# One decoder step: sample attention by column groups, and a pre-norm stage by token tiles in an order fixed by hand

## The chip, the cores and the metric

The kernel runs on one core of one Trainium2 chip. The metric is the device time of one execution in microseconds (us). Shown are three runs of the kernel before, and one more execution that the hardware profiler recorded.

## The reference

One layer of a hybrid decoder is applied to 256 prompt tokens (one sequence) and to 8 sample tokens (8 sequences with one new token each). Cut to what matters here:

```python
def rms_norm(x, w):
    y = x * lax.rsqrt(jnp.mean(x * x, axis=-1, keepdims=True) + EPS)
    return y * w

def window_attn_sample(q, k_new, v_new, cache_k, cache_v, sink):   # 8 sequences, 1 token each
    kc = jnp.concatenate([cache_k, k_new], axis=1)                 # 128 cached keys and the new one
    vc = jnp.concatenate([cache_v, v_new], axis=1)
    ...                                                            # mask: the 128 last keys
    scores = jnp.einsum('bqkgd,bskd->bkgqs', qg, kc) * (HEAD_DIM ** -0.5)
    p = sink_softmax(scores, mask, sink)                           # softmax with one sink per head
    return jnp.einsum('bkgqs,bskd->bqkgd', p, vc)

def decoder_layer(x, pos, lw, state):
    mix, new_state = token_mixers(rms_norm(x, lw['norm_mix_pre']), pos, lw, state)
    h = x + rms_norm(mix, lw['norm_mix_post'])
    f = swiglu_ffn(rms_norm(h, lw['norm_ffn_pre']), lw['w_gate_up'], lw['w_down'])
    return h + rms_norm(f, lw['norm_ffn_post']), new_state
```

`token_mixers` projects the normed input with `w_in` (2048 rows), runs the state-space branch (causal convolution, chunked scan) and the attention branch (32 query heads, 8 key heads of 64), projects both back with `w_ssm_branch` (4096 rows) and `w_attn_branch`, gates them, and applies `w_out`.

## The kernel before

Activations lie transposed: features on the 128 partitions, the T = 264 tokens (256 prompt, 8 sample) in the free dimension. Every projection is `gemm` (L146 to L190). A float32 operand is split in a high part (rounded to fp32r) and the low remainder, and each block of 128x128 weights is multiplied three times: high weights by high input (L186), high by low (L187), low by high (L188). For each 4 row blocks of 128, `gemm` loads a `raw` tile (1 MB, 3 buffers) from SP's queue, ScalarE copies it to `hi` (L176, 4 buffers) and VectorE subtracts to `lo` (L177, 4 buffers), two row blocks to an instruction; the products accumulate in 4 PSUM banks over all row blocks. After each such 4 row blocks `tick()` advances side work, written as generators, by a fixed rate. Each engine works in the order of its own queue; a tile scheduler sets that order at build time from the dependencies and its own estimate of durations.

**The start.** `x_sample`, the identity matrix and `norm_mix_pre` and the two prompt tiles `xt` of 128 tokens x 2048 (L216 to L223) are issued from SP's queue; constants and small vectors from POOL's (L225 to L238), the large constant table `cst` among them (L231). ScalarE squares `xt2` and `xt0` with an accumulated sum, VectorE `xt1` (L259 to L265). For each of the 16 chunks c of 128 features, TensorE transposes the three token tiles into one bank (L272), ScalarE copies it to `xr` (L274), and SP's queue stores it to `xT_d` for use much later (L275). `rsqrt` (L98) is a chain of small VectorE instructions; its result is spread over the partitions by a product with the identity (`rowcast`, L251) and copied to `rbx` (L280). Then for each chunk VectorE makes `xf` (L283), ScalarE the high part `XH[c]` (L92) and, for all 16 chunks, POOL the low part `XL[c]` (L93, `x0g`). The first `gemm`, of 512 columns of `w_in` at `C_B`, is written at L397; the second, of the 128 columns at `C_DT`, in `decays` (L328), and the third at `C_C`.

**Sample attention.** It is a side generator of the `w_ssm_branch` stage (L812 to L822; the queue of POOL also carries that stage's loads of `ts` and stores of `m1_d`). It takes the 8 sequences in two halves of four. For each sequence (L722 to L740): load the key window `kr` and the values `vb` from POOL's queue, transpose `kr` in 4 blocks (L732), copy to `kt` (L734), put in the new key (L735), and multiply, for each of the 4 blocks c, `kt` as the stationary operand by the 8 query columns of `QB` (L738); ScalarE copies the 32 score columns to `sT` (L739). Then for the half: transpose `sT` (L742), softmax over the free dimension (L746 to L754), transpose back (L756), multiply `vb`'s blocks as stationary operands by 8 columns of probabilities each (16 products, L763), and copy the result in 32 small pieces to the attention output `AF_` (L769). The pool `attn_s` that holds these tiles is opened before the attention stage (L531) and its `kr` buffers also serve the stores of new keys and values (L637 to L647).

```python
for c in range(4):
    PE.matmul(pS[:, c * 8:c * 8 + 8], kt[:, c, :], QB[:, b, c, :], start=True, stop=True)      # L738
...
PE.matmul(po[:, sl], Vb[bb][:, c * P:(c + 1) * P], pt[:, sl], start=True, stop=True)           # L763
```

Of the kernel before, what the change touches and what calls it, by code (L numbers as in the profile page):

```python
# [32 lines left out]
def build(tc, I, O, wbufs=(3, 4, 4), gbufs=5, sbufs=((3,), (1,), (3,)), woff=0, aux="gpsimd", rr=1.4, pr=1.2, su=2, sr=1.0, hb=5, xbb=2, x0g=(0, 1, 2, 3), x0st="sync"):  # L33
# [56 lines left out]
    def split(src, hi, lo, scale=None, E=None):  # L90
        if scale is None:
            S.copy(hi, src)  # L92
# [32 lines left out]
    side = []  # L125
    last = [None]
# [19 lines left out]
    def gemm(W, segs, nk, X, perm_heads=False, perm_rows=False):  # L146
# [4 lines left out]
        for g0 in range(0, nk, 4):  # L151
            raw = til(wp, [P, 4, 512], "raw", wbufs[0])
            with tc.high_priority(offset=woff):
# [11 lines left out]
                for b in range(2):  # L165
# [3 lines left out]
                    if perm_heads:  # L169
                        for k in range(2):  # L170
# [3 lines left out]
                            V.tensor_tensor(lk, rk, fr(hk), ALU.subtract)  # L174
                    else:
# [3 lines left out]
            for b in range(2):  # L179
                hi, lo = hl[b]  # L180
                for m in range(nch):
                    for k in range(2):
# [3 lines left out]
                        PE.matmul(ps[m][:, :T], wh, XH[kc], start=f, stop=False)  # L186
# [28 lines left out]
    xts = {}  # L215
    N1 = til(A0, [P, P], "N1")  # L216
    for t in (2, 0, 1):
        n = NS if t == 2 else P
        xts[t] = til(A0, [P, D], f"xt{t}")
        dma(xts[t][:n], I["x_prompt"][t * P:t * P + P] if t < 2 else I["x_sample"])  # L220
        if t == 2:
            dma(ident, I["consts"][:, 0:P])
            dma(N1[0:16], I["norm_mix_pre"].rearrange("(c p) -> c p", p=P))  # L223
# [7 lines left out]
    ld(cst, I["consts"][:, P:])  # L231
# [15 lines left out]
    ps = sps()  # L247
    PE.transpose(ps[:, 0:16], N1[:16], ident[:16, :16])
    V.tensor_copy(w_pre, ps[:, 0:16])

# [6 lines left out]
    ss = til(cp, [P, 3], "ss")  # L257
    V.memset(ss, 1.0)
    for t in (2, 0, 1):  # L259
        n = NS if t == 2 else P  # L260
        sq = til(A0, [P, D], "sq", 2)
        if t == 1:
            V.tensor_tensor_reduce(sq, xts[t], xts[t], 1.0, 0.0, ALU.mult, ALU.add, ss[:, t:t + 1])
        else:
            S.activation(sq[:n], xts[t][:n], AF.Square, accum_out=ss[:n, t:t + 1])  # L265
    X0G = x0g
    X0ST = getattr(nc, x0st).dma_start
    xrs = []
    for c in range(16):
        ps = sps()  # L270
        for t, n in enumerate((P, P, NS)):
            PE.transpose(ps[:, t * P:t * P + n], xts[t][:n, c * P:(c + 1) * P], ident[:n, :n])  # L272
        xr = til(A0, [P, T], "xr", 16)
        S.copy(xr, ps[:, :T])  # L274
        X0ST(xT_d[c], xr)  # L275
        xrs.append(xr)
    rbx = til(A0, [P, T], "rbx")
    with tc.high_priority():
# [836 lines left out]
```

## Time and profile before

| | |
|---|---|
| median of 3 runs | 2171.52 us (2171.44 to 2175.14) |
| profiled execution | 2174.78 us |
| span of its instructions | 2173.0 us |
| TensorE busy (PE) | 2134.5 us, 98% |
| VectorE (DVE) | 1380.0 us, 64% |
| ScalarE (ACT) | 1105.6 us, 51% |
| GpSimd (POOL) | 275.5 us, 13% |
| DMA, mean over the span | 204 GB/s |

The profiled execution is 3.3 us above the median, and 1.8 us longer than the span of its instructions. Busy time is the union of an engine's instructions; matmuls are pipelined, so that one row of TensorE lasts longer than the distance to the next one's start. A float32 product shows as two rows of TensorE, a transpose and an fp32r product as one. The trace gives the granted TensorE clock from its first event on, here 31.63 us; for earlier times the views print 1.00, and the durations of equal products tell the clock there.

### The profile page before, as it was taken

What the parts mean: (1) busy time and instruction counts of PE and PEld (TensorE: products, weight loads), DVE (VectorE), ACT (ScalarE), POOL (GpSimd) and SP (SyncE); (2) the same over time, 40 slices, a digit from 0 to 9 for tenths busy, and PEclk for the clock granted to TensorE, in tenths of its full rate; (3) what the DMA queues carried; (4) which work ended last, traced back from release to release, by engine and by line L of the source; (5) the groups of instructions that cost most, each with busy time, mean ns of one, the idle gap of its engine ahead of it and who ended that gap; (6) DMA issues with size and microseconds to landing.
All of it is one profiled execution on the core that took longest, in us unless ns stands there. A gap on an engine that the chain in (4) does not pass through costs nothing.

```text
span 2173.0 us, 43304 instructions
## 1 busy us (share of the span) xinstructions
PE 2134.5 (98%) x17533; PEld 2103.9 (97%) x17533; DVE 1380.0 (64%) x2764; ACT 1105.6 (51%) x1984; POOL 275.5 (13%) x512
## 2 busy tenths in 40 slices
PE   8999999999999999999999999899999999999997
PEld 6999999999999999999999999899999999999997
DVE  5877776777689988866544554844554545544444
ACT  5555555555478977755433444544444444434442
POOL 4100111111133222223001120300000000000000
PEclk9999999999999999999999999999999999999998
DMA  5655665555587787877567985365655555565552
GB/s 194 230 184 191 197 195 181 190 189 190 176 308 244 251 284 260 287 228 234 173 198 190 219 261 183 118 212 189 208 189 187 194 195 185 180 225 178 175 175 99
DMA packets 216633, 442.52 MB, mean 204 GB/s; under 512 B 12352, under 2 KB 28240, under 8 KB 215656
## 3 DMA queue, kind: packets, MB, share of 16 engines
q1 hardware_dynamic: 194864, 372.51, 53.2%
q0 software_dynamic: 21424, 67.17, 9.4%
q8 instruction: 137, 2.24, 0.4%
q14 instruction: 64, 0.52, 0.1%
q10 hardware_dynamic: 144, 0.07, 0.0%
HBM read 402.81 MB, written 41.45 MB: 204 GB/s over the span
## 4 chain that ended last, share of the span: by engine, by line
PE 91%; DMA 4%; DVE 3%; issue 1%; ACT 1%; POOL 0%; SPq 0%; DVEq 0%; ACTq 0%; POOLq 0%
PE g L186 28%; PE g L188 28%; PE g L187 28%; DMA raw<-in_w_attn_branch 2%; DMA y<-y_d 1%; PE s L272 1%; DVE lo L177 1%; PE w L701 1%; PE w L662 0%; PE w L694 0%; DMA ta_d<-tg 0%; DMA xt<-in_x_prompt 0%; ACT hi L176 0%; PE s L467 0%; DMA ts_d<-tg 0%
## 5 line engine op out<-in xcount | busy, mean ns | idle before, releaser
L177 DVE TENSOR_TENSOR lo<-raw,hi 128x1024 fp32r<-128x1024 f32 (+1 forms) x640 | 776.9, 1217 | 594.4 <-ACT hi L176 588.0
L176 ACT CAST hi<-raw 128x1024 fp32r<-128x1024 f32 (+1 forms) x640 | 663.6, 1040 | 850.7 <-PE g L187 767.7
L186 PE MATMUL g<-XH,hi 128*128 128x264 f32 x2192 | 630.8, 289 | 3.6 <-ACT tg L789 1.8
L187 PE MATMUL g<-XL,hi 128*128 128x264 f32 x2192 | 628.1, 287 | 0.0
L188 PE MATMUL g<-XH,lo 128*128 128x264 f32 x2192 | 626.1, 288 | 0.1
L186 PEld LDWEIGHTS g<-XH,hi 128*128 128x128 f32 x2192 | 413.9, 189 | 7.7 <-ACT tg L789 2.5
L187 PEld LDWEIGHTS g<-XL,hi 128*128 128x128 f32 x2192 | 414.2, 189 | 4.0 <-issue 3.5
L188 PEld LDWEIGHTS g<-XH,lo 128*128 128x128 f32 x2192 | 413.3, 189 | 3.5 <-issue 2.0
L187 PE MATMUL g<-HL,hi 128*128 128x264 f32 x1408 | 398.5, 285 | 2.1 <-DVE HL L908 2.1
L188 PE MATMUL g<-HH,lo 128*128 128x264 f32 x1408 | 397.6, 285 | 0.1
L186 PE MATMUL g<-HH,hi 128*128 128x264 f32 x1408 | 392.8, 286 | 1.8 <-ACT HH L901 1.8
L187 PEld LDWEIGHTS g<-HL,hi 128*128 128x128 f32 x1408 | 267.0, 190 | 3.0 <-DVE HL L908 3.0
L188 PEld LDWEIGHTS g<-HH,lo 128*128 128x128 f32 x1408 | 264.8, 189 | 0.4 <-DVE lo L177 0.3
L186 PEld LDWEIGHTS g<-HH,hi 128*128 128x128 f32 x1408 | 261.4, 188 | 1.8 <-ACT HH L901 1.8
L186 PE MATMUL g<-FH,hi 128*128 128x264 f32 x704 | 201.3, 286 | 0.0
L188 PE MATMUL g<-FH,lo 128*128 128x264 f32 x704 | 200.8, 286 | 0.0
L187 PE MATMUL g<-FL,hi 128*128 128x264 f32 x704 | 200.0, 284 | 0.0
L186 PE MATMUL g<-YH,hi 128*128 128x264 f32 x512 | 148.4, 292 | 0.9 <-ACT YH L92 0.9
L187 PE MATMUL g<-YL,hi 128*128 128x264 f32 x512 | 148.4, 290 | 0.7 <-DVE YL L93 0.7
L188 PE MATMUL g<-YH,lo 128*128 128x264 f32 x512 | 148.4, 290 | 0.0
L186 PEld LDWEIGHTS g<-FH,hi 128*128 128x128 f32 x704 | 132.9, 189 | 0.0
L188 PEld LDWEIGHTS g<-FH,lo 128*128 128x128 f32 x704 | 132.5, 188 | 0.0
(415 smaller groups left out, 3021.4 us busy)
## 6 DMA issues: line engine op xcount, KB each, us to landing
raw<-in_w_in SPq DMA_DIRECT2D x136, 1024.0 KB, 5.3
raw<-in_w_gate_up SPq DMA_DIRECT2D x88, 1024.0 KB, 5.0
raw<-in_w_down SPq DMA_DIRECT2D x44, 1024.0 KB, 5.1
raw<-in_w_ssm_branch SPq DMA_DIRECT2D x32, 1024.0 KB, 5.2
h<-in_state_ssm POOLq DMA_DIRECT2D x64, 256.0 KB, 5.3
out_ssm_sample<-h POOLq DMA_DIRECT2D x64, 256.0 KB, 4.9
raw<-in_w_attn_branch SPq DMA_DIRECT2D x32, 512.0 KB, 10.7
raw<-in_w_out SPq DMA_DIRECT2D x16, 1024.0 KB, 5.1
```

The lines of the kernel that those rows point to most:

```text
L176: S.copy(hi[:, :, :w], r)
L177: V.tensor_tensor(lo[:, :, :w], r, fr(hi[:, :, :w]), ALU.subtract)
L186: PE.matmul(ps[m][:, :T], wh, XH[kc], start=f, stop=False)
L187: PE.matmul(ps[m][:, :T], wh, XL[kc], start=False, stop=False)
L188: PE.matmul(ps[m][:, :T], wl, XH[kc], start=False, stop=l)
L272: PE.transpose(ps[:, t * P:t * P + n], xts[t][:n, c * P:(c + 1) * P], ident[:n, :n])
L701: PE.matmul(pw[jj[j], q, 384:512], Vk[:, k, vc[j]], pT[j][:, (q + k) * P:(q + k + 1) * P], start=f, stop=l)
```

## The change

It has two parts.

**The start.** The prompt is loaded in four pieces of 128x1024 as the first four DMAs of SP's queue; `x_sample`, the identity and `norm_mix_pre` are issued from ScalarE's queue; the table `cst` is issued from SP's queue after the first gemm is written. A tile `wz` of zeros is made by POOL. The pre-norm stage is written inside `manual_schedule` for TensorE, ScalarE and VectorE, whose instructions then keep the order written: 7 products of zeros (`busy(7)`), the transposes of token tile 0 in groups of four chunks to one bank, those of the 8 sample tokens, those of token tile 1, 3 products of zeros, the 3 that spread the `rsqrt` result (now transposes of a broadcast operand, left in PSUM), 2 products of zeros. VectorE copies tile 0's banks and ScalarE tile 1's, into one tile `XR`; the squares are taken over half tiles. `XR` is stored to `xT_d` by 4 DMAs from POOL's queue. The low parts `XL` are subtracted on VectorE; in the first gemm `issue_after` ties each `hi` and `lo` to the chunk that it is to follow in the queue.

**Sample attention.** The scores are computed with the queries as the stationary operand (`QP`, 32 columns, of which 8 are in use and 24 zero) and the keys `kt` as the moving one, the block c into partitions 32c to 32c+31: the scores come out with heads on the partitions, for four sequences in one bank, which stays until the softmax has read it. The products with the values take the 32 probability columns of a sequence as the stationary operand and all 512 value columns as the moving one, sequence bb into partitions 32bb to 32bb+31. Four transposes per half then bring the result to the attention layout, copied in 8 pieces. A yield stands between softmax and values and another before the last transposes. The tiles come from a new pool `attn_w` that is opened after the attention stage's pools are released (L856 of the changed kernel).

```diff
-            (E or V).tensor_tensor(lo, src, fr(hi), ALU.subtract)
+            return a, (E or V).tensor_tensor(lo, src, fr(hi), ALU.subtract)
...
+    wz = til(A0, [P, NP], "wz")
+    G.memset(wz, 0.0)
...
+    for t in range(2):
+        for c0 in range(0, D, XC):
+            dma(xts[t][:, c0:c0 + XC], I["x_prompt"][t * P:t * P + P, c0:c0 + XC])
+    S.dma_start(xts[2][:NS], I["x_sample"])
+    S.dma_start(ident, I["consts"][:, 0:P])
+    S.dma_start(N1[0:16], I["norm_mix_pre"].rearrange("(c p) -> c p", p=P))
...
-    ld(cst, I["consts"][:, P:])
...
+        def busy(n):
+            for _ in range(n):
+                PE.matmul(pw[:, 0:NP], wz[:, 0:P], wz, start=True, stop=True)
...
+        busy(7)
+        S.activation(sq[:NS], xts[2][:NS], AF.Square, accum_out=ss[:NS, 2:3])
+        for h in range(2):
+            S.activation(sq[:, h * XC:h * XC + XC], xts[0][:, h * XC:h * XC + XC], AF.Square, accum_out=s4[:, h:h + 1])
+            for k in (2 * h, 2 * h + 1):
+                V.tensor_copy(*turn(0, k))
...
+        V.tensor_tensor_reduce(sv2, xts[1][:, XC:], xts[1][:, XC:], 1.0, 0.0, ALU.mult, ALU.add, s4[:, 3:4])
...
+        busy(3)
+        rs = rsqrt(cp, [(lambda a: a, ss)], P, 3, 1.0 / D, EPS, "rx")
...
+        busy(2)
...
-        X0ST(xT_d[c], xr)
...
+        st(xT_d[c:c + 4].rearrange("c p t -> p c t"), XR[:, c:c + 4, :])
...
-        split(xf, XH[c], XL[c], E=G if c % 4 in X0G else V)
+        a, b = split(xf, XH[c], XL[c])
+        first[0][c + 1] = a.ins
+        first[1][c - 1] = b.ins
+
+    pss0 = gemm(win, [(C_B, 512)], 16, (XH, XL), behind=first)
+    dma(cst, I["consts"][:, P:])
...
-                    PE.matmul(pS[:, c * 8:c * 8 + 8], kt[:, c, :], QB[:, b, c, :], start=True, stop=True)
-                S.copy(sT[:, 32 * bb:32 * bb + 32], pS[:, 0:32])
+                    PE.matmul(pS[32 * c:32 * c + 32, bb * P:(bb + 1) * P], QP[:, bb, c, :], kt[:, c, :], start=True, stop=True)
...
-                for c in range(4):
-                    sl = slice(bb * 32 + c * 8, bb * 32 + c * 8 + 8)
-                    PE.matmul(po[:, sl], Vb[bb][:, c * P:(c + 1) * P], pt[:, sl], start=True, stop=True)
...
+                PE.matmul(po[32 * bb:32 * bb + 32, :], pt[:, bb].rearrange("p c r -> p (c r)"), Vb[bb], start=True, stop=True)
...
+                PE.transpose(ps[:, c * P:(c + 1) * P], pc[:, c * P:(c + 1) * P], ident)
...
+    SB = pool("attn_w")
     side.append([sample_attention(), sr, 0.0])
```

How TensorE's queue begins in the kernel before (s and g are PSUM banks, xt_42 and xt_43 the prompt's token tiles, xt_41 the sample's):

```order
L248 MATMUL s_160<-ident_67,N_40_131 128x16
L272 MATMUL s_171<-ident_67,xt_42_136 128x128
L272 MATMUL s_178<-ident_67,xt_42_136 128x128
L272 MATMUL s_185<-ident_67,xt_42_136 128x128
L272 MATMUL s_171<-ident_67,xt_43_138 128x128
L272 MATMUL s_171<-ident_67,xt_41_132 128x8
```

and in the changed kernel (xt_41 and xt_42 are the prompt's tiles, xt_43 the sample's, wz the zeros; of the four groups of each prompt tile the first and the last are shown):

```order
L275 MATMUL s_171<-wz_131 128x256 x7
L280 MATMUL g_181<-ident_67,xt_41_133 128x128 x4
L280 MATMUL g_200<-ident_67,xt_41_133 128x128 x4
L292 MATMUL s_206<-ident_67,xt_43_135 128x8 x16
L280 MATMUL g_227<-ident_67,xt_42_134 128x128 x4
L280 MATMUL g_247<-ident_67,xt_42_134 128x128 x4
L275 MATMUL s_171<-wz_131 128x256 x3
L307 MATMUL g_272<-ident_67,rxy_258 128x128 x2
L307 MATMUL g_272<-ident_67,rxy_258 128x8
L275 MATMUL s_171<-wz_131 128x256 x2
L192 MATMUL g_347<-XH_4_86,hi_353 128x264
```

Zero products stand ahead of the transposes and around the spreading, and the transposes go token tile by token tile instead of chunk by chunk.

VectorE's queue at the beginning of the first gemm, in the changed kernel:

```order
L315 SCALAR_TENSOR_TENSOR xf_283<-XR_165,w_pre_158,g_272 128x264
L315 SCALAR_TENSOR_TENSOR xf_287<-XR_165,w_pre_158,g_272 128x264
L315 SCALAR_TENSOR_TENSOR xf_291<-XR_165,w_pre_158,g_272 128x264
L93 TENSOR_TENSOR XL_5_87<-xf_283,XH_4_86 128x264
L93 TENSOR_TENSOR XL_7_89<-xf_287,XH_6_88 128x264
L180 TENSOR_TENSOR lo_354<-raw_351,hi_353 128x1024
L315 SCALAR_TENSOR_TENSOR xf_295<-XR_165,w_pre_158,g_272 128x264
L315 SCALAR_TENSOR_TENSOR xf_299<-XR_165,w_pre_158,g_272 128x264
L93 TENSOR_TENSOR XL_9_91<-xf_291,XH_8_90 128x264
L93 TENSOR_TENSOR XL_11_93<-xf_295,XH_10_92 128x264
L180 TENSOR_TENSOR lo_358<-raw_351,hi_357 128x1024
```

The subtractions XL, which stood on POOL before, now alternate with xf and lo on VectorE, two chunks to one lo.

TensorE's queue where the `w_ssm_branch` stage begins, in the changed kernel (kw is a window of keys, kt its transposed copy, QP the queries; of the three products with YH the first is shown):

```order
L196 MATMUL g_12383<-XH_34_116,lo_12565 128x264
L775 MATMUL s_12932<-ident_67,kw_12930 128x128 x4
L192 MATMUL g_12852<-YH_1817_12638,hi_12858 128x264
L780 MATMUL s_12929<-kt_12937,QP_12914 32x128 x4
L775 MATMUL s_13004<-ident_67,kw_13002 128x128 x4
L195 MATMUL g_12852<-YL_1818_12639,hi_12858 128x264
```

The first score products now stand after the stage's first three products with YH; before, they stood after 48 of them.

## Rows read from the trace of the kernel before

**Rows 1.** The page: busy time of each engine, its share, instructions.
```profile
PE 2134.5 (98%) x17533; PEld 2103.9 (97%) x17533; DVE 1380.0 (64%) x2764; ACT 1105.6 (51%) x1984; POOL 275.5 (13%) x512
```

**Rows 2.** Windows, gemm banks only: start:end, length, PE busy (x rows), others, clock, DMA.
```profile
958.50:1022.79 64.29, 53.54 (x385) 51.47 (x385) 1.27 (x3) 0.66 (x2) 0.92 0.70 232
1022.79:1078.49 55.70, 49.85 (x387) 48.79 (x385) 1.37 (x4) 0.00 (x0) 0.97 0.51 165
1078.49:1172.22 93.73, 93.73 (x770) 93.73 (x769) 3.23 (x9) 0.00 (x0) 1.00 0.66 201
26.36:52.96 26.60, 26.26 (x193) 25.74 (x194) 0.00 (x0) 0.87 (x4) 1.00 0.31 90
52.96:61.16 8.20, 6.37 (x50) 5.89 (x48) 0.48 (x1) 0.86 (x4) 1.00 0.62 216
```

**Rows 3.** Timeline of TensorE, 0 to 34 us: start, length, instruction, idle time before.
```profile
11.52 6.81 PE L272 MATMUL s<-ident,xt 128*128 128x128 f32 x24 [3.09 <-DMA xt<-in_x_prompt]
...
26.36 1.25 PE L186 MATMUL g<-XH,hi 128*128 128x264 f32 x4
...
30.83 0.42 PE L188 MATMUL g<-XH,lo 128*128 128x264 f32 x1
...
33.92 0.28 PE L186 MATMUL g<-XH,hi 128*128 128x264 f32 x1
```

**Rows 4.** Timelines of VectorE, ScalarE and POOL: the start, and near 950 us.
```profile
11.62 2.29 DVE L263 CUSTOM_DVE_ANT_0 sq<-xt 128x2048 f32<-128x2048 f32 x1 [7.12 <-DMA xt<-in_x_prompt]
...
16.01 0.16 DVE L115 SCALAR_TENSOR_TENSOR rxy<-rxt,rxy 128x3 f32<-128x3 f32 x1
...
16.54 1.99 ACT L176 CAST hi<-raw 128x1024 fp32r<-128x1024 f32 x2 [0.26 <-DMA raw<-in_w_in]
...
20.38 2.35 DVE L177 TENSOR_TENSOR lo<-raw,hi 128x1024 fp32r<-128x1024 f32 x2
...
22.65 1.30 DVE L283 SCALAR_TENSOR_TENSOR xf<-xr,w_pre,rbx 128x264 f32<-128x264 f32 x3
...
34.79 1.77 DVE L177 TENSOR_TENSOR lo<-raw,hi 128x1024 fp32r<-128x1024 f32 x1
...
945.35 0.33 POOL L807 COPY rb<-RSB 128x8 f32<-128x8 f32 x2 [12.87 <-DVE RSB L587]
...
959.30 2.83 DVE L93 TENSOR_TENSOR YL<-y,YH 128x264 fp32r<-128x264 f32 x8
```

**Rows 5.** Timeline of TensorE in sample attention; first and last of 12 rows at 143 us.
```profile
143.33 0.44 PE L467 MATMUL s<-bc,X 128*64 128x128 f32 x4
...
145.79 0.39 PE L471 MATMUL s<-bc,X 128*64 128x128 f32 x4
...
957.01 0.60 PE L732 MATMUL s<-ident,kr 128*128 128x128 f32 x4
958.50 0.62 PE L186 MATMUL g<-YH,hi 128*128 128x264 f32 x3 [0.89 <-ACT YH L92]
...
966.90 0.95 PE L738 MATMUL s<-QB,kt 128*128 128x8 f32 x8
...
1005.31 0.30 PE L756 MATMUL s<-ident,pe 128*128 128x128 f32 x1 [1.23 <-DVE pe L754]
...
1008.26 4.08 PE L763 MATMUL s<-spt,vb 128*128 128x8 f32 x32
```

**Rows 6.** Timeline of TensorE at 138 us: a 512-column product, then the next row.
```profile
138.34 1.02 PE L433 MATMUL s<-X,Bk 128*128 128x512 f32 x2
138.79 0.69 PE L187 MATMUL g<-XL,hi 128*128 128x264 f32 x1
```

**Rows 7.** Windows, all instructions: busy by engine (PE, PEld, DVE, ACT, POOL), granted clock, DMA.
```profile
960.06:963.47 3.41, 3.41 (x17) 3.41 (x17) 2.08 (x7) 1.70 (x6) 1.60 (x2) 0.50 0.80 259
1011.26:1018.09 6.83, 6.83 (x33) 6.83 (x33) 2.36 (x9) 2.83 (x10) 3.59 (x7) 0.50 0.66 185
1052.22:1055.63 3.41, 3.41 (x18) 3.41 (x17) 2.66 (x12) 3.12 (x11) 0.00 (x0) 0.50 0.00 0
```

More of the change, by code (lines that the diff above doesn't have):

```diff
@@ L144, in drain, with gemm @@
                 side.remove(e)
-    def gemm(W, segs, nk, X, perm_heads=False, perm_rows=False):
+    def gemm(W, segs, nk, X, perm_heads=False, perm_rows=False, behind=None):
         XH, XL = X
@@ L174, in gemm @@
                             V.tensor_tensor(lk, rk, fr(hk), ALU.subtract)
+                    elif behind is not None:
+                        with tc.issue_after(behind[0][g0 + 2 * b]):
+                            S.copy(hi[:, :, :w], r)
+                        with tc.issue_after(behind[1][g0 + 2 * b]):
+                            V.tensor_tensor(lo[:, :, :w], r, fr(hi[:, :, :w]), ALU.subtract)
                     else:
@@ L281, in build @@
+    for c in range(0, 16, 4):
+        st(xT_d[c:c + 4].rearrange("c p t -> p c t"), XR[:, c:c + 4, :])
+    first = {0: xr_end.ins}, {}
     for c in range(16):
@@ L294, in build @@
     ps = sps()
-    PE.transpose(ps[:, 0:48], VR[:48], ident[:48, :48])
+    with tc.issue_after(mm0[16]):
+        PE.transpose(ps[:, 0:48], VR[:48], ident[:48, :48])
     V.tensor_copy(vecs, ps[:, 0:48])
@@ L395, in build @@
             for nm, c0 in (("B", C_B), ("C", C_C)):
-                with tc.issue_after(rb_end.ins):
-                    pss = gemm(win, [(c0 + g * P, 512)], 16, X)
+                pss = pss0 if g == 0 and nm == "B" else gemm(win, [(c0 + g * P, 512)], 16, X)
                 for i in range(4):
@@ L528, in build @@
     AFp = pool("attn_f")
-    AF_ = [til(AFp, [P, T], f"AF{c}") for c in range(16)]
+    AFb = til(AFp, [P, 16, T], "AF")
+    AF_ = [AFb[:, c, :] for c in range(16)]
     A4 = pool("attn_k")
@@ L752, in sample_attention @@
+            pe = til(SB, [P, 4, P], "pe", 1)
+            for bb in range(4):
+                S.activation(pe[:, bb, :], pS[:, bb * P:(bb + 1) * P], AF.Exp, bias=mx[:, bb:bb + 1], scale=0.125, accum_out=dn[:, bb:bb + 1])
             V.tensor_tensor(dn, dn, ek, ALU.add)
             V.reciprocal(dn, dn)
-            V.tensor_scalar(pe, pe, dn, None, ALU.mult)
+            V.tensor_tensor(pe, pe, dn.unsqueeze(2).broadcast_to([P, 4, P]), ALU.mult)
+            yield
             ps = sps(1)
-            PE.transpose(ps[:, 0:P], pe, ident)
@@ new lines, in sample_attention @@
+            S.copy(pc, po[:, :])
+            yield
+            ps = sps(1)
+            for c in range(4):
+                PE.transpose(ps[:, c * P:(c + 1) * P], pc[:, c * P:(c + 1) * P], ident)
+            for c in range(4):
+                pv = ps[:, c * P:(c + 1) * P].rearrange("p (b c j i) -> p c j i b", b=4, c=4, j=2)[:, c]
+                for j in range(2):
+                    jj = slice(64 * j, 64 * j + 64)
+                    (S.copy if j else V.tensor_copy)(AFb[jj, 4 * c:4 * c + 4, NP + 4 * b4:NP + 4 * b4 + 4], pv[jj, j])
@@ L821, in build @@
             drain()
+            SB.release()
             SA.release()
```

130 lines of the change are left out of this document (66 added, 64 removed).

## The prediction
> **What bounds the kernel now.** I read the page first: TensorE is busy for 98% of the span [rows 1]. So a change is worth what it takes off TensorE's own queue, and I next looked where that queue is worse than its best pace. Windows of the gemm banks alone give the pace: in the second half of the `w_ssm_branch` stage 770 rows take 93.73 us, 0.1217 us each, with nothing between [rows 2]. Three stretches are worse. The first gemm takes 26.60 us for 193 rows, and starts only at 26.36 us. The stretch 958.50 to 1022.79 holds 385 gemm rows that are worth 46.9 us, and takes 64.29; the next holds 387, worth 47.1, and takes 55.70. That is 17.4 + 8.6 = 26.0 us which go to sample attention, its waits, and a lower clock. The changed parts sit in exactly these stretches. What follows them (1078 to 1172 us) runs at pace, so what is saved ahead stays saved.
>
> The start, in the timeline: TensorE waits for the prompt until 11.52 us, then 24 transposes take 6.81 us, 0.284 each [rows 3]. VectorE squares for 2.29 us from 11.62 on and ends the chain of `rsqrt` at 16.17 [rows 4]. The gemm's products begin at 26.36. At 30.83 one still lasts 0.42 us, at 33.92 it is 0.28 [rows 3]: of the two levels this is 1.2 GHz and then 2.4, and the trace's first granted clock stands at 31.63.
>
> **The start, changed.** Three small DMAs leave SP's queue ahead of the prompt, and `cst` (128x1368 float32, 0.70 MB) no longer loads beside it; tile 1 was there at 11.52, I take 9.5 as an estimate, with SP starting about 1.3 us earlier. Only half a tile is squared after that: 1.15 us. Adding the partial sums is one more small instruction, 0.2; `rsqrt` took 2.3 us from the end of the squares (13.91 to 16.17). So the statistics are ready near 13.4.
>
> TensorE must have the transposes behind it by then. It has 32 wide and 17 narrow ones. At the start's 0.284 each they take 13.9 us; at the pace of four in 0.60 us at 957 [rows 5], an average of 0.15 at most, 7.4 us, largely while the prompt still lands. Zero products: a 512-column float32 product has its two rows 0.45 us apart with the next [rows 6], so one of 256 columns takes 2 x 0.22 = 0.45 us at 2.4 GHz, 0.9 at 1.2. Seven of them cover roughly 1 to 7 us, when TensorE would idle anyway; they cost nothing unless the first piece and the identity land earlier, and then at most 2 us. The three and the two near the spreading cost 1.3 + 0.9 us at 2.4 GHz, most of it under `rsqrt` and under the first `xf`; at 1.2 GHz twice that, 2.2 of it on the path.
>
> What the products of zeros buy is the clock: I take it to be high for a part of the start, so that the spread result is there at 16.5 instead of 13.6 (all high) or 24 (all low: 7 + 13.9 + 2.7 + 0.8). Then the first gemm. VectorE needs for two chunks 2 x 0.43 (`xf`), 2 x 0.36 (`XL`, by the eight in 2.83 us) and 1.18 (`lo`) = 2.76 us [rows 4]; TensorE needs 24 x 0.1217 = 2.92. So TensorE stays just the bound: first `lo` at 16.5 + 3.2, sixteen products behind it, seven more groups of 2.92: 16.5 + 3.2 + 1.9 + 20.4 = 42.0, and 1.5 for a group at low clock: 43.5. Before, it ended at 52.96 [rows 2]. **Term: -9.5 us**, bounds -14 (13.6, no low clock) and -2 (24).
> The first weights landed at 16.54 before [rows 4]; with less ahead of them they are there in time. `XR`'s four stores wait in POOL's queue, behind which nothing is due before the first convolution. The `hi` casts, 1 us each [rows 4], stand behind tile 1's copies on ScalarE and are due with the spread result. The second gemm (8.20 us for 48 products) waits for its `raw` buffers, which its own small blocks hold; that stays as it is: 0.
>
> A rule speaks against the middle of this. The row first: from 11.52 to 26 us TensorE issued transposes all but without a pause, and the products after them still ran at 1.2 GHz [rows 3]. The Trainium skill (TensorE: Matmul & The Clock Gate, Part 4: PE-mode transpose) states that transposes do not count as busy for the clock in the way products do. By that, the clock would be lost again during the transposes, and the first rival below would be the case.
>
> **Sample attention, changed.** *Scores.* Eight groups of 8 rows; one took 0.95 us with the tail of its last row, and by 32 such rows in 4.08 us [rows 5] I count 0.86 to a group, 6.9 in all. Products that go to 64-column halves run two at a time: 48 rows from 143.33 to about 146.0, 0.056 each. Eight at that pace are 0.45, with four quarters at once 0.22; I take 0.3 a group, 2.4 in all: -4.5 (-3.3 to -5.1). *Values.* 32 rows in 4.08 us per half, 7.7 for both without tails. Now 8 rows of 512 columns per half: 0.22 a row if 64 columns are two at a time is the model, alone 0.45 [rows 6], so 3.6 per half alone and 0.9 four at a time; I take 1.1: -5.5 (-0.5 to -5.9). The Trainium skill (TensorEngine Tiling (Array Packing), Tiling Modes) gives four independent tiles for 128x32, and says that a change of mode drains the engine. By the first of these the values would take 0.9 per half; no run here shows four at once, and for the drain there is no price. *Transposes.* 12 more in all (two halves: 8 instead of 4 in the softmax, 8 new ones), four in 0.6 at most: +1.3 to 1.8. *Waits.* The transpose of the softmax waited 1.23 us for VectorE; it now stands behind a yield: -0.5 (0 to -1.2). At the head of the stage the first score products stand after three products with YH. They need `kt`, which ScalarE copies among its YH casts; TensorE waited there 0.89 us for YH. ScalarE has two casts, the copy and four more casts ahead of the last piece of `kt`; by VectorE's 0.35 for the same size [rows 4] that is over 2 us: +1.5 (0 to +3). Behind them stand all products with YL. *Clock.* In 1011.26 to 1018.09 and in 1052.22 to 1055.63 the granted clock is 0.5 [rows 7], behind the two runs of 32 products of 8 columns, the first at 1008.26 [rows 5]; 10.24 us at half pace lose 5.1. Those runs go: -5.1 (0 to -5.1). The stretch at 960.06 belongs to the head's waits and stays. **Term: -4.5 - 5.5 + 1.5 - 0.5 + 1.5 - 5.1 = -12.6 us**, bounds about 0 and -16.
>
> ScalarE and VectorE: 8 small copies per half instead of 32, off TensorE's path: 0. POOL: `vb`, then `kw`, then three `ts` loads stand in its queue after the attention pools' last readers; at 945 us POOL had been idle for 12.87 us before [rows 4], and the keys are due at 957: 0, unless the pool's release comes late.
>
> **Sum.** -9.5 - 12.6 = -22.1 against the profiled execution's 2174.8: 2152.7. That execution is 3.3 above the median, so **2149.5 us**.
>
> **The rivals.**
> 1. *A cold start.* The clock falls again during the transposes, the later zero products run at 1.2 GHz, and the spread result comes near 24: the first term is -2 and the time 2157. For it: the transposes before did not raise the clock. Against: part of them follow seven products directly.
> 2. *Column groups do not overlap.* Scores stay at -3.3 or worse, values at -0.5, the clock falls in one of the two halves after all: the second term is about -4, the time 2158.
> 3. *Slower.* In the first three gemms VectorE, with XL on it now, feeds TensorE in such small portions that the clock is not granted until the third ends: 432 products at 0.22 instead of 0.1217 cost 42 us, 34 above what the start gains. Price: 2149.5 + 42 = 2191.5. It decides if VectorE needs more than 24 x 0.22 = 5.3 us for two chunks. Even with a `lo` at 1.77 us, as beside POOL's work [rows 4], it needs 3.4, so at 1.2 GHz TensorE has work without gaps, as it had around 30.83 before [rows 3]. That speaks against it.
> 4. *Nothing at all:* the time gained at the start is lost at the second gemm's wait for weights, and the clock's stretches come at other places: within 4 us of before.
>
> **How the numbers follow.** Chances: forecast 0.66, rival 1 0.19, rival 2 0.09, rival 3 0.03, rival 4 0.03. A difference under 0.2%, 4.3 us, can hardly be told from none. The forecast and rivals 1 and 2 are all faster by more: 0.94; same 0.03; slower 0.03. For the range I take the forecast with its terms' bounds short of their extremes (-32.5 to -9.5 against the median), and both faster rivals: 2139 to 2162.
>
> **What would show it.** Right: gemm products from about 17.5 us and the first gemm's end near 43; rows of 0.28 us from its second group on; no granted clock of 0.5 after the value products; score groups under 0.45 us, values near 1 us per half; 385 gemm rows of the stage's first quarter in 53 to 56 us. Wrong: a first product after 22 us, or value rows 0.45 us apart (rivals 1, 2); long waits of TensorE for `lo` before 60 us (rival 3); a wait of TensorE for `kw` at the head of the `w_ssm_branch` stage would add what I put at nothing.

## The result, and the profile after

| | before | changed |
|---|---|---|
| median | 2172.23 us (4 runs) | 2148.9 us (4 runs, 2147.63 to 2150.49) |
| ratio, 95% interval | | 0.9891 (0.9873 to 0.9908) |
| profiled execution, span | 2174.78, 2173.0 us | 2147.96, 2146.2 us |

The forecast was 2149.5 us. The change is faster by 23.3 us between the medians and by 26.8 between the two profiled spans (the one before lies above its median, the one after below). Four more runs of the changed kernel, beside the last experiments, gave 2150.49 us against 2172.44, a ratio of 0.9896 (0.9883 to 0.9910).

The page of the changed kernel, busy time of each engine:

```profile
PE 2115.9 (99%) x17518; PEld 2084.1 (97%) x17518; DVE 1376.0 (64%) x2759; ACT 1103.3 (51%) x1960; POOL 261.6 (12%) x504
```

TensorE's timeline at the start, which answers to [rows 3] (start, length, instruction, count, in brackets the idle time before and its releaser):

```profile
1.10 6.06 PE L275 MATMUL s<-wz 128*128 128x256 f32 x14 [1.10 <-POOL wz L224]
7.00 1.91 PE L280 MATMUL g<-ident,xt 128*128 128x128 f32 x16
8.93 1.13 PE L292 MATMUL s<-ident,xt 8*128 8x8 f32 x16
9.99 1.97 PE L280 MATMUL g<-ident,xt 128*128 128x128 f32 x16
11.79 1.46 PE L275 MATMUL s<-wz 128*128 128x256 f32 x6
14.60 0.55 PE L307 MATMUL g<-ident,rxy 128*128 128x128 f32 x3 [1.35 <-DVE rxy L115]
15.08 1.13 PE L275 MATMUL s<-wz 128*128 128x256 f32 x4
16.27 0.74 PE L192 MATMUL g<-XH,hi 128*128 128x264 f32 x4
```

Fourteen rows of zeros in 6.06 us are 0.43 us each: 1.2 GHz. The six at 11.79 are 0.24 each: 2.4 GHz. The trace's first granted clock is 1.00 at 6.75 us, where the kernel before had it at 31.63. The sixteen transposes of a token tile take 1.91 us, 0.12 each, where the 24 of [rows 3] took 0.284 each. The first product of the gemm starts at 16.27 instead of 26.36.

VectorE's timeline of the same stretch, the two rows that set its end:

```profile
10.78 1.23 DVE L298 CUSTOM_DVE_ANT_0 sv<-xt 128x1024 f32<-128x1024 f32 x1 [0.65 <-DMA xt<-in_x_prompt]
14.29 0.16 DVE L115 SCALAR_TENSOR_TENSOR rxy<-rxt,rxy 128x3 f32<-128x3 f32 x1
```

The last half tile's squares waited for its transfer until 10.78, and the `rsqrt` chain ended at 14.45.

Windows of the gemm banks alone, as in [rows 2] (TensorE's busy time and rows, its weight loads, VectorE, ScalarE, granted clock, DMA):

```profile
16.27:42.05 25.78, 24.49 (x193) 23.69 (x193) 6.09 (x14) 0.49 (x3) 1.00 0.61 218
42.05:49.86 7.81, 6.28 (x50) 5.85 (x48) 0.48 (x1) 1.17 (x6) 1.00 0.67 228
943.82:998.63 54.81, 49.32 (x384) 47.97 (x385) 1.28 (x3) 0.77 (x2) 0.97 0.80 255
998.63:1051.96 53.33, 49.67 (x386) 47.45 (x385) 0.84 (x2) 0.00 (x0) 1.00 0.59 194
1051.96:1145.49 93.53, 93.53 (x771) 93.53 (x769) 3.85 (x10) 0.00 (x0) 1.00 0.66 204
```

The two stretches that hold sample attention now take 54.81 and 53.33 us; they took 64.29 and 55.70: 11.85 us less. The stretch behind them runs at pace in both.

TensorE's timeline in that stage: the head, then one score group, the softmax's transposes, the value products and the last transposes of a half, as [rows 5] showed them before.

```profile
942.33 0.60 PE L775 MATMUL s<-ident,kw 128*128 128x128 f32 x4
943.82 0.64 PE L192 MATMUL g<-YH,hi 128*128 128x264 f32 x3 [0.89 <-ACT YH L92]
946.01 0.65 PE L780 MATMUL s<-kt,QP 128*32 128x128 f32 x8 [1.56 <-issue]
946.59 1.11 PE L775 MATMUL s<-ident,kw 128*128 128x128 f32 x4
947.36 0.57 PE L195 MATMUL g<-YL,hi 128*128 128x264 f32 x1
...
966.74 0.43 PE L780 MATMUL s<-kt,QP 128*32 128x128 f32 x8
...
992.13 0.60 PE L798 MATMUL s<-ident,pe 128*128 128x128 f32 x4
...
996.32 1.07 PE L803 MATMUL s<-vb,spt 128*32 128x512 f32 x8
...
1000.46 0.60 PE L809 MATMUL s<-ident,pc 128*128 128x128 f32 x4
```

The second half's value products in the kernel before, which ran at a clock of 1.00:

```profile
1047.41 3.63 PE L763 MATMUL s<-spt,vb 128*128 128x8 f32 x32
```

Rows overlap, so I count what a group displaces: the distance from the gemm row ahead of it to the one behind it, less the 0.122 us that two gemm rows are apart anyway. By that a score group costs 0.45 us (0.81 before), the value products of a half 1.08 (3.49 for these 32 rows before), four transposes 0.36.

The granted clock behind the values is 1.00: there is no stretch of 0.50 between 948.82 and 1341.36 us, where the kernel before had 6.83 and 3.41 us [rows 7]. The stretch at the head stays (all instructions; TensorE, weight loads, VectorE, ScalarE, POOL, clock):

```profile
945.41:948.82 3.41, 2.81 (x18) 2.46 (x19) 3.41 (x9) 2.20 (x9) 3.41 (x1) 0.50 0.71 152
```

### The profile page after: what moved, and what is told of

The parts are those of the page before. It is cut to its first block, busy times and chain, and to the rows that moved or that the text cites. A ratio compares the mean times of both kernels' runs of the same rounds, so it can differ in the third digit from the quotient of the medians.

```text
span 2146.2 us, 43210 instructions
## 1 busy us (share of the span) xinstructions
PE 2115.9 (99%) x17518; PEld 2084.1 (97%) x17518; DVE 1376.0 (64%) x2759; ACT 1103.3 (51%) x1960; POOL 261.6 (12%) x504
## 4 chain that ended last, share of the span: by engine, by line
PE 93%; DMA 3%; DVE 2%; issue 1%; ACT 1%; SPq 0%; POOL 0%; DVEq 0%; ACTq 0%; POOLq 0%
PE g L192 29%; PE g L196 29%; PE g L195 29%; DMA raw<-in_w_attn_branch 1%; PE w L740 1%; DMA out_ssm_sample<-h 1%; PE w L733 0%; PE w L701 0%; DMA xt<-in_x_prompt 0%; PE s L504 0%; DMA raw<-in_w_in 0%; DVE HL L954 0%; PE s L475 0%; PE s L462 0%; PE s L508 0%
## 5 line engine op out<-in xcount | busy, mean ns | idle before, releaser
L183 DVE TENSOR_TENSOR lo<-raw,hi 128x1024 fp32r<-128x1024 f32 (+1 forms) x632 | 765.3, 1214 | 592.2 <-ACT hi L182 590.0
L196 PE MATMUL g<-XH,lo 128*128 128x264 f32 x2192 | 619.6, 287 | 1.2 <-DVE lo L180 0.7
L196 PEld LDWEIGHTS g<-XH,lo 128*128 128x128 f32 x2192 | 408.7, 188 | 4.7 <-issue 1.9
L195 PEld LDWEIGHTS g<-FL,hi 128*128 128x128 f32 x704 | 133.1, 189 | 0.0
## 6 DMA issues: line engine op xcount, KB each, us to landing
raw<-in_w_attn_branch SPq DMA_DIRECT2D x32, 512.0 KB, 10.1
```

What stands on the lines that cost most here:

```text
L183: V.tensor_tensor(lo[:, :, :w], r, fr(hi[:, :, :w]), ALU.subtract)
L195: PE.matmul(ps[m][:, :T], wh, XL[kc], start=False, stop=False)
L196: PE.matmul(ps[m][:, :T], wl, XH[kc], start=False, stop=l)
```

## The experiments

The theory in short: two independent gains, a start that is 11 to 13 us shorter because the clock is high and the prompt's transposes lie under its transfer, and sample attention that is 12 us shorter because its products are fewer rows side by side and no longer cost the clock.

**Each part alone.** The first kernel is the one before with the start's edits (everything in the diff ahead of the attention stage), the second the one before with the rest.

> The kernel before with the new start alone (the sample attention stays as it was). My theory: the first gemm ends about 11 us earlier (42.05 against 52.96 us), the stretch of low clock at 62.35 us, in the third gemm, goes too (2.4 us), so 13 us faster than the kernel before, and the two stretches at clock 0.50 in the w_ssm_branch stage stay. The prediction on record gave the start 9.5 us. A rival, that the start's gain is given back later and only the two parts together gain: under 5 us.

> The kernel before with the new sample attention alone (the start stays as it was). My theory: 12 us faster than the kernel before (on record 12.6), the clock stays at 1.00 behind the value products, and the dip at 62.35 us is still there. If this and the start alone do not add up to the changed kernel's 23 us within 3 us, the two parts act on each other.

The start alone: 2159.2 us against 2172.53, ratio 0.9939 (0.9927 to 0.9951), 13.3 us. Sample attention alone: 2160.72 us, ratio 0.9948 (0.9935 to 0.9962), 11.8 us. Together 25.1, against 23.3 and 22.0 for the two series of the changed kernel: the parts add up within the uncertainty. With the start alone the clock is again 0.50 for 3.41 us from 999.66 and from 1037.20 us, behind the old value products. With sample attention alone it is 1.00 there, and 0.50 for 3.41 us from 61.08, as before from 62.35.

The `w_ssm_branch` stage by itself, from its first product with `YH` to the first product of the next projection, takes 213.73 us before, 210.48 with the start alone, 202.39 with sample attention alone, and 201.67 in the changed kernel. So the same old sample attention took 3.3 us less in the profile of the start alone: the transpose behind the softmax displaced 0.03 us there instead of 1.44, and the clock was low for 3.41 us behind the first values instead of 6.83. That much of sample attention's gain hangs on the execution and the schedule that one starts from.

**The changed kernel once more.** No edit.

> The changed kernel once more, on the chip of the next three, to have its spread and its clock in a second profile. Both theories: near 2149 us. Of the granted clock: if it is set by the instructions alone, the profile has 1.00 from about 6.7 us to the head of the w_ssm_branch stage as in the first one; if the same waits sometimes cost the clock and sometimes not, dips near 16.9 or 51 us may show, as they did in the runs with the start alone and with one column group, whose start is the same, and the time varies by 2 to 3 us.

2150.49 us (2148.99 to 2151.14). The second profile has two stretches of low clock that the first had not:

```profile
16.71:20.13 3.42, 3.19 (x15) 2.84 (x14) 3.42 (x8) 2.48 (x4) 0.00 (x0) 0.50 1.04 411
50.85:54.26 3.41, 3.41 (x17) 3.41 (x17) 3.41 (x6) 2.50 (x4) 0.10 (x1) 0.50 0.97 350
```

The same instructions, but the first gemm ends at 42.86 us instead of 42.05 and the third at 75.63 instead of 73.64: 2.0 us between two executions, in which the clock is what differs. The first low stretch follows TensorE's wait for the `rsqrt` chain, the second its waits in the second gemm. The Trainium skill (TensorE: Matmul & The Clock Gate, Part 1) states that how much of a kernel runs slow at its start varies from run to run. Here the slow start itself hardly varied (the clock is granted from 6.75 and from 6.47 us on); what varied is whether the clock fell again later. So a difference of 2 us between two profiles says nothing here unless the stretch that it comes from is shown.

**Without the products of zeros.**

```diff
-        busy(7)
...
-        busy(3)
...
-        busy(2)
```

> The changed kernel without its twelve products of zeros. My theory (they buy the clock): the transposes run at 1.2 GHz, 32 wide ones at 0.28 and 17 narrow ones in some 2 us from 7 us on, the spread result comes near 19 us, the first gemm runs its first 5 us at 1.2 GHz: 4 to 6.5 us slower than the changed kernel. Rival A (the transposes by themselves raise the clock within a few us): 1 to 2 us slower. Rival B (the statistics' chain sets the start anyway, and the clock is granted by time): within 1 us.

2151.51 us, but from 2146.84 to 2159.95; ratio 0.9908 (0.9890 to 0.9925). The profiled execution was the slowest of the six. TensorE's timeline there:

```profile
7.24 3.65 PE L280 MATMUL g<-ident,xt 128*128 128x128 f32 x16 [7.24 <-DMA ident<-in_consts]
10.94 1.85 PE L291 MATMUL s<-ident,xt 8*128 8x8 f32 x16
12.72 3.55 PE L280 MATMUL g<-ident,xt 128*128 128x128 f32 x16
16.11 0.53 PE L305 MATMUL g<-ident,rxy 128*128 128x128 f32 x3
18.20 0.75 PE L192 MATMUL g<-XH,hi 128*128 128x264 f32 x4 [1.56 <-ACT XH L92]
20.15 0.59 PE L196 MATMUL g<-XH,lo 128*128 128x264 f32 x1 [0.71 <-DVE lo L180]
20.54 0.42 PE L192 MATMUL g<-XH,hi 128*128 128x264 f32 x1
```

The transposes run at 0.23 us each, 1.2 GHz; the first gemm begins 1.9 us later than with the zeros. The granted clock is 1.00 from 16.01 and 0.50 again from 19.42 to 26.25, and the first gemm ends at 46.68, 4.6 us later than in the first profile of the changed kernel and 3.8 later than in the second. (The rest of the 12 us by which this execution is above the first profile arises far from the edit: near 1180 and 1231 us TensorE waits 6.5 us for `ts`, 3.0 in the changed kernel, and the clock is low for 3.41 us from 1179.95 and from 1231.15.) By the end of the third gemm, at 78.03 us, it is 4.4 us behind the first profile of the changed kernel and 2.4 behind the second. So in profiles the zeros are worth 2.4 to 4.4 us, where the theory had 4 to 6.5; over the runs the median is 1.0 to 2.6 us above the changed kernel's two, and the fastest run is as fast as any of them. That is nearer to rival A, and the reason is in the rows: nothing but transposes ran from 7.24 us on, and the clock was granted at 16.01. Transposes did raise it, only late. The zeros bring the grant forward to a time when TensorE has nothing else to do.

Most of the start's gain does not come from the zeros: without them the gemm's first product still stands at 18.20 us, 8.2 of the 10.1 us earlier. The transposes begin at 7.24 us instead of 11.52 and end at 16.27 instead of 25.74, at the lower clock in both kernels. Which of the order of the loads, the order by token tile and the halved squares gives how much of this, no run separates.

**The first seven alone** (without `busy(3)` and `busy(2)`).

> The changed kernel with the first seven products of zeros and without the three and two near the spreading. My theory (the clock, once granted at 6.75 us, outlasts the wait of 12 to 16 us, in which those five stand): within 1 us of the changed kernel. Rival (without them TensorE has 3 rows between 12 and 16.3 us, the clock falls, and the first gemm begins at 1.2 GHz): 2 to 3.5 us slower, with first gemm products 0.42 us long.

2151.71 us (2151.19 to 2153.59), ratio 0.9906 (0.9893 to 0.9919), 1.2 to 2.8 us above the changed kernel. Its profile has the clock at 0.50 from 16.86 and from 51.00 us, the same two stretches as the second profile of the changed kernel, and its third gemm ends at 75.81 us against 75.63 there. So with like clocks the five later zeros are worth nothing that shows (0.2 us). Whether they make the low stretch rarer these runs don't settle: of the ten profiles that have all twelve zeros, three have a stretch of 0.50 beginning between 16.6 and 17.0 us. The transposes behind the seven zeros, from 7.34 to 12.3 us, ran at a clock of 1.00 throughout.

**The old value products in the changed kernel.**

```diff
-                PE.matmul(po[32 * bb:32 * bb + 32, :], pt[:, bb].rearrange("p c r -> p (c r)"), Vb[bb], start=True, stop=True)
+                for c in range(4):
+                    sl = slice(bb * 32 + c * 8, bb * 32 + c * 8 + 8)
+                    PE.matmul(po[:, sl], Vb[bb][:, c * P:(c + 1) * P], pt[:, bb, c, :], start=True, stop=True)
```

> The changed kernel with the values multiplied as before: per half 16 products of 8 columns (32 rows) in one run, no transposes behind them. My theory: 32 rows cost 4.1 us per half where the new ones cost 1.08, less 0.36 for the four transposes: 5.3 us in all; and behind each run the clock falls as before (3.4 and 1.7 us at half pace lost): 10.4 us slower than the changed kernel. Rival (the dips had another cause, such as the wait of 1.23 us for the softmax): 5.3 us slower, clock 1.00 behind the values.

2155.93 us, ratio 0.9926 (0.9914 to 0.9939): 5.4 to 7.0 us slower than the changed kernel. The two runs of 32 rows displaced 3.49 and 4.12 us. With the second the clock fell, while it still ran; behind the first it did not:

```profile
998.00:1002.00 4.00, 4.00 (x38) 4.00 (x37) 1.46 (x3) 0.00 (x0) 2.27 (x5) 1.00 0.91 304
1041.40:1044.20 2.80, 2.80 (x28) 2.80 (x27) 0.72 (x1) 0.00 (x0) 0.00 (x0) 1.00 0.60 234
1044.20:1051.03 6.83, 6.83 (x33) 6.83 (x33) 4.36 (x12) 4.98 (x15) 0.00 (x0) 0.50 0.00 0
```

So neither expectation holds whole. The profiled execution is 8.0 us above the first profile of the changed kernel (2155.93 against 2147.96): 5.3 for the rows, as both had it, and up to 3.4 for one low stretch of 6.83 us; the theory's 10.4 needed a fall with both runs.

Over the three profiles with unbroken runs (before, the start alone, this one) the clock fell in five of these six runs or within 1.2 us behind them; in the nine profiles with the new value products, behind none of eighteen. That the runs of small products are the cause is argued from these counts. TensorE counts as busy for all of 1041.40 to 1051.03 in the windows, so that column does not tell a reader that the clock is at risk; what stands ahead of the fall are rows of 8 columns.

**The old value products, spread** (a `yield` behind each sequence's eight rows).

> As the kernel with the old values, but the 32 rows of a half in four pieces of 8, a yield between them, so that gemm products stand between. My theory (it is the unbroken run of small products after which the clock falls): no clock of 0.50 there, 5.3 us slower than the changed kernel. Rival (small products cost the clock wherever they stand): 10 us slower, or more.

2154.85 us, ratio 0.9923 (0.9911 to 0.9936). That is 4.4 to 6.0 us above the changed kernel, near the theory's 5.3. The clock answers for one half only: the scheduler put the first half's four pieces as 16 rows at 998.18, 8 at 1001.18 and 8 at 1009.47, with few gemm rows between the first two, and the clock was 0.50 from 1002.05 to 1005.46. In the second half they stood as four pieces of 8, from 1060.43 to 1076.10, and the clock stayed at 1.00. That fits the unbroken run as the cause, on one half.

**One column group.** The values of all four sequences go to the same partitions, so that the result of three is left out.

```diff
+            V.memset(po, 0.0)
...
-                PE.matmul(po[32 * bb:32 * bb + 32, :], ...
+                PE.matmul(po[0:32, :], ...
```

> The changed kernel with the value products of all four sequences of a half put into the same 32 partitions (the last one stays, the other three sequences' results are left out and the rest of the bank is zero). My theory (the four run at once because they stand in four column groups): 8 rows of 512 columns one after the other, 0.22 to 0.45 us each, 1.8 to 3.6 us per half instead of 1.08: 1.4 to 5 us slower than the changed kernel. Rival (the products would overlap anyway, 32 columns being a quarter of the array): no change.

2156.79 us, ratio 0.9932 (0.9918 to 0.9945), 6.3 to 7.9 us slower than the changed kernel. TensorE's rows:

```profile
998.81 3.62 PE L804 MATMUL s<-vb,spt 128*32 128x512 f32 x8
...
1042.54 3.62 PE L804 MATMUL s<-vb,spt 128*32 128x512 f32 x8
```

The same eight rows take 3.62 us in one group and 1.07 in four: 0.45 us each, and four at a time. Two halves make 5.1 us. In one group the eight rows cost TensorE as much as the 32 old ones (3.64 us displaced against 3.49), so the column groups are what makes the new value products cheap. This is the upper bound that the prediction had from [rows 6], and the rival "column groups do not overlap" made to happen. My own expectation, 1.4 to 5 us, was too small: the profile has the two low stretches near the start too, from 16.91 and 51.04 us, and its third gemm ends 2.3 us later than in the first profile of the changed kernel, at 75.99; the `w_ssm_branch` stage takes 207.53 us, 5.9 more. Behind these two runs of 3.62 us the clock stayed at 1.00, so a run's length alone is not what makes it fall.

**The keys later.** The transposes of each key window are tied behind the gemm products written ahead of them.

```diff
-                for c in range(4):
-                    PE.transpose(ps[:, c * P:(c + 1) * P], kr[:, c * P:(c + 1) * P], ident)
+                with tc.issue_after(mmL[0]):
+                    for c in range(4):
+                        PE.transpose(ps[:, c * P:(c + 1) * P], kr[:, c * P:(c + 1) * P], ident)
```

(`mmL[0]` is the last product that `gemm` has written.)

> The changed kernel with the transposes of each key window tied behind the gemm products written before them, so that at the head of the w_ssm_branch stage no score product stands ahead of the products with YL. My theory (TensorE's 1.84 us wait there is for kt, copied behind the YH casts on ScalarE): the wait goes, 1.5 to 2 us faster than the changed kernel, and up to 1.7 more if the clock's dip at 945.41 us goes with it. Rival (YH and YL are late themselves): the wait moves to the first products with YL, within 0.7 us of the changed kernel.

2151.84 us, ratio 0.9911 (0.9897 to 0.9925): no gain. TensorE's timeline at the head:

```profile
944.45 0.63 PE L193 MATMUL g<-YH,hi 128*128 128x264 f32 x3 [1.32 <-ACT YH L92]
947.19 0.51 PE L196 MATMUL g<-YL,hi 128*128 128x264 f32 x1 [2.10 <-DVE YL L93]
947.49 0.42 PE L197 MATMUL g<-YH,lo 128*128 128x264 f32 x1
```

The wait moved to `YL`, as the rival said. What stands ahead of `YL` on VectorE, in the changed kernel and then in the kernel before:

```profile
940.55 1.23 DVE L183 TENSOR_TENSOR lo<-raw,hi 128x1024 fp32r<-128x1024 f32 x1 [1.69 <-ACT hi L182]
941.70 3.32 DVE L854 SCALAR_TENSOR_TENSOR y<-y,sv,rb 128x264 f32<-128x264 f32 x8
944.93 1.23 DVE L183 TENSOR_TENSOR lo<-raw,hi 128x1024 fp32r<-128x1024 f32 x1
946.06 2.84 DVE L93 TENSOR_TENSOR YL<-y,YH 128x264 fp32r<-128x264 f32 x8
```

```profile
947.66 1.70 DVE L810 SCALAR_TENSOR_TENSOR y<-y,sv,rb 128x264 f32<-128x264 f32 x4
949.44 1.23 DVE L177 TENSOR_TENSOR lo<-raw,hi 128x1024 fp32r<-128x1024 f32 x1
950.59 1.70 DVE L810 SCALAR_TENSOR_TENSOR y<-y,sv,rb 128x264 f32<-128x264 f32 x4
```

In the changed kernel the eight scalings of `y` stand between the third and the fourth low part of this stage. In the kernel before they stood ahead of the first and the second, and TensorE waited 0.67 us for `YL`. The change does not touch that line; the scheduler moved it.

**The keys later and `y` earlier.** `issue_after` ties the first two `lo` of the stage behind the scalings.

> The kernel with the keys later, and with VectorE's eight scalings of y put back ahead of the first four low parts of the w_ssm_branch stage, where they stood in the kernel before. Theory formed on the last runs: at the stage's head TensorE waits for YL (2.10 us with the keys later), which is late because those scalings (3.32 us) stand between the low parts in VectorE's queue: the wait falls to about 0.7 us, 1.4 us faster than with the keys later, and 1.5 us faster than the changed kernel. Rival (YL waits for the YH casts of ScalarE): no change against the keys later.

2157.54 us, ratio 0.9935 (0.9922 to 0.9947): slower by 7 us. At the head the theory held in part: TensorE no longer waited for `YL`, but waited 1.53 us ahead of the fourth product with `YH`, for ScalarE's `tg`, so that `YL`'s first product came 2.39 us after YH's first (946.65 and 949.04), instead of 2.74:

```profile
948.81 0.39 PE L197 MATMUL g<-YH,hi 128*128 128x264 f32 x1 [1.53 <-ACT tg L839]
```

And the next two groups of `y` came late, and with them everything behind (VectorE, then TensorE):

```profile
959.80 1.71 DVE L861 SCALAR_TENSOR_TENSOR y<-y,sv,rb 128x264 f32<-128x264 f32 x4 [5.94 <-DMA y<-y_d]
```

```profile
963.93 0.66 PE L786 MATMUL s<-kt,QP 128*32 128x128 f32 x8 [3.40 <-issue]
```

VectorE waited 5.94 us for `y`'s transfer, and TensorE 3.40 at a score group: its `kt` is copied by ScalarE behind `YH` casts that need this `y`. The wait was moved, not removed.

**Products in two more waits.** In the head of the feed-forward part, four products of 256 columns on constants behind the token sums, three behind the spreading.

```diff
+        fill(4)
         r1 = rsqrt(cp, [(f, f(ps)) for f in halves], P, 3, 1.0 / D, 4 * EPS, "r1")
         rb1 = rowcast(r1, sps())[:, :T]
+        fill(3)
```

> The changed kernel with products on constants, used by nobody, put in two more waits: four of 256 columns behind the sums of squares ahead of the feed-forward part (TensorE waits 2.53 us there for the rsqrt chain) and three behind the spreading (2.11 us for HH). Theory (filled waits keep the clock): the stretch at 0.50 from 1341.36 us on (6.83 us, 3.4 us lost) goes: 3 us faster than the changed kernel. Rival A (the clock is lost to the small products of one column ahead of the wait, or at another place of the same head): no change. Rival B (the products delay the spreading or the first gemm products): up to 1 us slower.

> The last two together: keys later, y earlier, and the two filled waits. If both theories hold: 4.5 us faster than the changed kernel, near 2144.5 us. If neither: as the changed kernel.

The fill alone: 2152.39 us, ratio 0.9906 (0.9892 to 0.9919). All three edits: 2155.48, ratio 0.9925 (0.9912 to 0.9937). Beside them the changed kernel took 2150.49: no gain in either (the kernel with all three holds the edits to the keys and `y`, which cost 7 us by themselves). In the first the clock fell in spite of the fill, from 1345.05 to 1351.87, after the 1.40 us of fill at 1343.60 (windows of the kernel with the fill alone):

```profile
1343.60:1345.00 1.40, 1.40 (x12) 1.24 (x9) 1.06 (x8) 0.00 (x0) 0.00 (x0) 1.00 0.56 123
1345.05:1351.87 6.82, 6.82 (x22) 5.34 (x21) 4.78 (x15) 2.38 (x6) 1.68 (x4) 0.50 0.33 126
```

Ahead of the fill stand 30 rows with one column each, which fits rival A. With all three edits the clock stayed at 1.00, and still nothing was gained: from the first product with `w_out` to the first with `w_down` the changed kernel takes 627.83 us and this one 627.64. The windows of that kernel show why (TensorE, weight loads, VectorE first):

```profile
1352.00:1380.00 28.00, 24.27 (x180) 22.47 (x179) 28.00 (x49) 19.05 (x38) 21.77 (x29) 1.00 0.23 76
```

VectorE is busy for all 28 us and feeds TensorE with `HL`, for which TensorE waits 2.9 us there and 2.2 in the changed kernel. In the fourteen profiles of all these kernels the stretch takes 627.64 to 628.98 us, whether the clock at the head of the feed-forward part is low for 0, 6.83 or 10.24 us: the clock there shows no effect on the time. No version here beats the changed kernel.

## Why the prediction was right

**The start, predicted -9.5.** Alone it gave -13.3 by the runs; the first gemm ended at 42.05 and 42.86 us in the two profiles, against 52.96: -10.9 and -10.1. So the term was 0.6 to 1.4 us too small for the first gemm, and too small besides by what the other two gave. By its steps:

- The statistics were to be ready near 13.4 and were at 14.45 (the step's own terms add up to 13.15): the last piece of the prompt was there at 10.78, not at 9.5; the `rsqrt` chain took 2.13 us from 12.32 on (2.3 predicted).
- The clock was to be high for a part of the start, and the spread result there at 16.5. It was high from 6.75 on, the transposes took 0.12 us each, and the result was there at 15.15. The two errors have opposite signs.
- From there to the end of the first gemm the step was 27.0 us (16.5 to 43.5), with 1.5 for a low clock. It was 26.9 in the first profile, in which the clock was high: the 1.5 was not lost, and the rest took 1.4 longer than the 25.5 reckoned. That the step came out is luck.
- The second gemm was put at 0, and the third left out of the sum. **This is the step that failed.** The third gemm ended at 73.64 and 75.63 us, against 87.39 before (1.7 to 2.8 us more than the first gemm's gain). Its low stretch at 62.35 followed the second gemm's waits; the changed kernel has it in one profile of two, and of the twelve profiles with the new start three have it, of the two with the old start both. So a part of this gain is a matter of the execution. The second gemm takes 7.81 us instead of 8.20.

**Sample attention, predicted -12.6.** Alone -11.8 by the runs, -11.85 in the two windows. By its steps, in displaced time:

| step | predicted | measured |
|---|---|---|
| scores | -4.5 (bounds -3.3 to -5.1) | 0.81 to 0.45 a group, eight groups: -2.9 |
| values | -5.5 | 3.49 to 1.08 a half: -4.8 |
| transposes | +1.5 | 0.03 to 0.36 and 0.36 more, per half: +1.4 |
| wait of the softmax | -0.5 | the first half's transpose displaced 1.44, all but 0.03 a wait, which is gone: -1.4 |
| head | +1.5 | from the first product with `YH` to the first with `YL`, 1.29 (958.50 to 959.79) to 3.54 (943.82 to 947.36), less the score group and the four transposes now between them: +1.4 |
| clock | -5.1 | 10.24 us at half pace gone: -5.1 |

These add up to -11.4; 0.45 of the windows' 11.85 is not assigned. The scores were mis-sized: I took 0.3 for a group between two and four at a time, and a group displaces 0.45. The clock's term came out by the profile before, with its 10.24 us; with the start alone the same old products had 6.82. Nor is it shown that the new yield took the softmax's wait away, since the old code with the new start had no such wait either. The head's size was right and its reason wrong: not `kt`, which the kernel with the keys later took out of the way at no gain, but `YL`, behind scalings of `y` that the scheduler had moved. With those put back TensorE did not wait for `YL`, but a wait for `tg` stood in its place.

**The sum.** -22.1 predicted, -23.3 and -22.0 measured between medians. But the sum was worked out on the profile before, and from that profile to the first of the changed kernel the gain is 26.8 (2174.78 to 2147.96). So its mechanisms hold in both large terms, and that the median was hit within 0.6 us is luck in part: on the same profiles the third gemm's 2.8, the first gemm's 1.4 and the softmax wait's 0.9 were missing, the scores and values gave 1.6 and 0.7 less, some 2 us are not assigned, and the profile before lies 2.6 us above its four runs' median while the one after lies 0.9 below its own. The range's lower end was not "short of the extremes": the bounds -14 and -16 add up to -30, and it took -32.5.

**The rivals.** The cold start did not happen. Its rule, that transposes do not count as busy for the clock (the Trainium skill, TensorE: Matmul & The Clock Gate, Part 4), is not borne out by the changed order: with the zeros ahead of them the clock stayed at 1.00 through 5 us of transposes, and without the zeros it was granted after 8.8 us of nothing else. The kernel before does agree with the rule, and why its transposes did not raise the clock is open: they came 0.284 us apart with 8-column ones among them, and no run tried that order. Without overlap in the column groups the values cost 5.1 us more, as the second rival supposed. VectorE never fed TensorE so thinly that the clock went (third rival): the longest wait for `lo` in the first gemm was 0.72 us. (Its 42 us would have been 32.5 above the start's 9.5, not 34.) The fourth, no gain at all, did not happen either: the time gained at the start was kept through the second gemm.

## What to carry to other kernels

Products on zeros cost nothing that shows where TensorE has nothing else to do, and whether they are worth having hangs on what bounds the next stage: in the start they bring the clock ahead of 49 transposes and a gemm and were worth 2.4 to 4.4 us by the profiles, 1.0 to 2.6 between medians of runs that spread more widely; in the feed-forward's head the same trick gave nothing, since VectorE set the pace. Small products whose output has few rows belong side by side in column groups, with the long side moving: 3.62 us in one group became 1.07 in four, and the runs of 8-column products, with which the clock had fallen in five cases of six, are gone. After any edit, look at what the scheduler moved on the other engines near it, and profile the same kernel twice before a difference of 2 us is explained.

## What the runs showed of the hardware

- Four products with 32 stationary columns each, in four column groups, run at once: 8 rows of 512 columns in 1.07 us, 3.62 in one group.
- The granted clock can differ between executions of the same instructions: low from 16.71 and from 50.85 us in one profile, high there in the other, 2.0 us by the end of the third gemm.
- Without the zeros, the clock was granted at 16.01 us after nothing but transposes from 7.24 us on. Behind seven products of zeros, transposes from 7.34 to 12.3 us ran at 1.00 throughout.
- Runs of 32 rows of 8 columns show TensorE as busy, and the clock was 0.50 in or shortly behind five of six of them; behind two runs of 3.62 us of 512-column rows it stayed at 1.00.
